# MLA attention: VectorE's work of the maxima in program order, their row on ScalarE's queue, their start one chunk later

## The chip, the cores and the metric

The kernel runs on one core of one Trainium2 chip. The metric is device time in microseconds from launch to end; the program is the same in each run. The profile is one execution of it, recorded on that core; its times count from the start of the span.

## What is computed

The kernel computes two layers over 2048 latent tokens with 256 context tokens ahead of them, width 1024: multi-head latent attention (MLA), then gated linear attention. The change lies in MLA, of which this is the part that matters:

```python
q = (rms_norm(cq, q_norm_g) @ w_uq).reshape(b, n, MLA_HEADS, MLA_NOPE + MLA_ROPE)      # 16 heads, 64 + 32
...
k = jnp.concatenate([k_nope, jnp.broadcast_to(kr, (b, n, MLA_HEADS, MLA_ROPE))], axis=-1)
...
s = jnp.einsum('bqhrd,bkhd->bhrqk', qi, k, preferred_element_type=F32) * scale
p = jax.nn.softmax(s, axis=-1).astype(v.dtype)
return jnp.einsum('bhrqk,bkhe->bqhre', p, v)
...
return (o.reshape(b, n, MLA_WIDTH) * jax.nn.silu(gate)) @ w_out
```

Context queries read the 256 context keys only; latent queries read all 2304 keys.

## The kernel before

**Tiling.** Heads go in 8 pairs, and each pair's queries in 5 chunks: the context (256 columns) and four of 512. `steps` lists the 40 (pair, chunk) in order, and `si` is an index in it. Keys come in tiles of 128, so an *item* (si, kt) is one tile of keys against one chunk of queries for two heads: 2 items for a context chunk, 18 for each other, 74 for a pair, 592 in all.

**The maxima run ahead.** Softmax needs each query's maximum before its scores are exponentiated. `maxima()` is a generator, advanced step by step: one step is four matmuls of 128 queries against up to 512 keys (L491) into two of the three PSUM banks of pool `pmp` (tile `pmx`) and two reductions on VectorE (L493) into the tile `mx`; a chunk of 512 columns takes 20 steps, a context chunk 2. When a chunk is complete, `close()` reduces `mx` to `mc` (L502, VectorE), transposes it on TensorE (L505), writes the negative as `mr` (L509, VectorE) and sends it with two small DMAs (L511) into row 32 of that chunk's query tile `qs`. There it is the 33rd row of the last of five terms of the scores, against a row of ones in the keys.

**Query up-projection (p2q, 535 to 690 us).** Five chunks, each of 8 pairs and 4 rope blocks; a block is nine matmuls into a `pj` bank. `feed()` advances the maxima here until 30 steps (`lead`) are done; its step `due` and the places that call it set where they fall. The function `fetch()` prepares the first query and key tiles between them: a DMA, then two GpSimd instructions that split the tile in a high and a low part (L48, L53).

**Attention (p3, 690 to 2366 us).** One loop over the items. Each item has `scores` (ten matmuls L628 into one of two PSUM tiles `st`, then Exp on ScalarE L630 into one slot of a ring of nine) and mostly one step of the maxima; one item in three prepares a key or query tile of what comes later. Behind each group of up to six items comes a *burst*: `thirds` sums three slots on VectorE in four instructions (L661), `values` multiplies the group's slots with `vt` (L677, 24 matmuls for six items), `finish` ends the chunk that was completed in the burst before (L692 on TensorE over the sums `acc`, Ln and Exp on ScalarE, a product on GpSimd, a DMA), `gated` (L683, VectorE) takes over the output of a chunk whose last group this was, and a chunk whose maxima are complete is closed: mc ahead of the thirds, the transpose and mr behind the values. GpSimd adds slots and sums up in `acc` (L651). In the last pair the loop also prepares the output weights `wo` (cast on ScalarE, low part on VectorE or GpSimd) and the first context output `o0h`, `o0l`.

**What sets the order.** A scheduler orders each engine's program. An instruction that went through `tc.keep_in_program_order` stays behind the one traced just before it on its engine; `pe_op` does this once `pinned` is set, at the start of p3. In p3 the matmuls, the reductions L493 and the thirds L661 are pinned; mc, mr and ob (L683) are not. DMAs wait in the program of the engine that issues them, in its order; those of L511 are issued by SyncE, as are the loads of qf, kf, gt and vt.

Of the kernel before, what the change touches and what calls it, by code (L numbers as in the profile page):

```python
# [10 lines left out]
F32 = mybir.dt.float32  # L11
F32R = mybir.dt.float32r
# [110 lines left out]
def body(ctx, tc, I, out, stop=99, dbg=None):  # L123
# [349 lines left out]
    def maxima():  # L473

        for si, (pr, ci) in enumerate(steps):
# [3 lines left out]
            qs = qss[si]  # L479
            mx = qsp.tile([P, 8, 5], F32, name="mx", bufs=2)  # L480
            kh = kb[pr % 2][0]
# [16 lines left out]
    def close(si, qs, mx, nq, npart):  # L498

        n = nq * P  # L500
        mc = qsp.tile([P, 8], F32, name="mc", bufs=2)
        nc.vector.reduce_max(mc[:, :2 * nq], mx[:, :2 * nq, :npart], axis=AX.X)  # L502
        yield
        pt = pmp.tile([P, 512], F32, name="pmx")
        pe_op(nc.tensor.transpose(pt[:2 * nq, :P], mc[:, :2 * nq], ident))  # L505
        yield
        closed.add(si)
        mr = qsp.tile([8, P], F32R, name="mr", bufs=2)
        nc.vector.tensor_scalar(mr[:2 * nq, :], pt[:2 * nq, :P], -1.0, None, op0=ALU.mult)  # L509
        for j in range(2):  # L510
            nc.sync.dma_start(qs[64 * j + 32:64 * j + 33, 1, 1, :n].bitcast(F32), mr[j * nq:j * nq + nq, :].bitcast(F32))  # L511

# [7 lines left out]
    with pool("p2q", 2) as sp, pool("ps2q", 5, space=PSUM) as psp:  # L520
# [20 lines left out]
        def feed():  # L541
            nonlocal fed, due
            due += 0.82
            while fed < min(due, lead):
                fed += 1
                next(stream, None)
                while closes:
                    for _ in closes.pop():
                        pass

        for ci, (c0, n) in enumerate(CHUNKS):
# [4 lines left out]
            if ci == 3:  # L556
                tasks.append((load_q, (2,)))
            for pr in range(NPAIR):
                if pr == 1 and ci + 1 < len(CHUNKS):
# [9 lines left out]
                store(qn_d[ci][pr], kk[:, :n])  # L569
                if ci >= 3 or (ci == 2 and pr >= 4):  # L570
                    feed()
            tab = sp.tile([P, 2, 512], F32, name="tabq", bufs=1)
            nc.sync.dma_start(tab[:, :, :n], I["tab"][:, :, c0:c0 + n])
            for g in range(2):
# [6 lines left out]
                for r in range(2):  # L581
# [6 lines left out]
                    store(qr_d[ci][4 * g:4 * g + 4, :, 16 * r:16 * r + 16, :].rearrange("q h d t -> (q h) d t"), t1[:, :n])  # L588
                    if ci >= 2:
                        feed()  # L590
                        feed()
# [8 lines left out]
    wo = {}  # L600
    tc.keep_in_program_order(nc.scalar.preload_act_table_set("natural_log_exp_and_others"))
    with pool("p3", 2) as sp, pool("ps3", 2, space=PSUM) as psp:
# [76 lines left out]
        def gated(si):  # L679
            n = CHUNKS[steps[si][1]][1]  # L680
            st_ = live[si]
            st_["ob"] = sp.tile([P, 512], F32, name="ob")
            nc.vector.tensor_tensor(st_["ob"][:, :n], st_["po"][:, :n], st_["gt"][:, :n], op=ALU.mult)  # L683

# [25 lines left out]
        def first_o():  # L710
# [3 lines left out]
            oh, ol = [qsp.tile([P, KT, P], F32R, name=f"o0{s}", tag="qf", bufs=2) for s in "hl"]  # L714
            k.hi("a", oh, of)
            k.lo("v", ol, of, oh)
            return oh, ol
# [24 lines left out]
        def out_weights(b, raw):  # L742
# [3 lines left out]
            for kt in range(4):  # L746
                k.hi("a", w2[0][:, kt, :], raw[kt])
                k.lo("p" if kt == 2 else "v", w2[1][:, kt, :], raw[kt], w2[0][:, kt, :])
                wo[4 * b + kt] = (w2[0][:, kt, :], w2[1][:, kt, :])
# [8 lines left out]

        def burst(i, end=False):

            nonlocal nv, nb, fed
            group = items[nv:i]
            nv = i
            nb += 1
# [25 lines left out]
        for i, (si, kt, nk) in enumerate(items):  # L790
# [19 lines left out]
            if i == len(items) - 30:  # L810
                o0 = first_o()
            if i and (items[i - 1][1] % 6 == 5 or items[i - 1][1] == items[i - 1][2] - 1):
                burst(i)
        burst(len(items))
        out_weights(1, raw)
# [747 lines left out]
```

## Time and profile before

| | us |
|---|---|
| median of 3 runs | 3736.59 |
| lowest, highest | 3736.35, 3737.76 |
| the profiled execution | 3737.41 |
| its span | 3735.6 |
| TensorE busy | 3539.5 |
| VectorE busy | 2283.1 |
| ScalarE busy | 1336.9 |
| GpSimd busy | 1405.8 |

The span is what the profile shows of an execution; 1.8 us of the profiled one lie outside it. In the rows, PE is TensorE's matmul, PEld its weight load, DVE VectorE, ACT ScalarE, POOL GpSimd, SP SyncE; SPq and ACTq are DMAs issued by these. A name as `pmx<-kbs,qs` reads output<-inputs, and L491 is line 491. An idle time in square brackets is that of the engine just before the row, with what released it. A row of windows is a stretch and its length, then busy time (and instructions) of PE, PEld, DVE, ACT and POOL, of PE and PEld alone where a line of TensorE's is picked, and then the granted clock of TensorE as a share of full speed, the busy share of the DMA engines, and GB/s.

### The profile page before, as it was taken

The numbers are of one execution on the slowest core, as the hardware profiler recorded it, in microseconds if no ns is written. First come the engines' busy times: TensorE is split into PE (matmuls) and PEld (weight loads), VectorE is DVE, ScalarE is ACT, GpSimd is POOL, SyncE is SP. The second block draws the span as 40 slices with busy tenths as digits, with TensorE's granted clock in tenths as the row PEclk, the third lists the DMA queues.
The fourth block names the chain that finished last, engine by engine and source line by source line (L and its number), as shares of the span: only waits on it lengthen the run. The fifth ranks groups of instructions, "written<-read, shape, count | busy, mean of one in ns | idle before, by whom it ended". The sixth has DMA issues, their size and how long they took to land.

```text
span 3735.6 us, 59336 instructions
## 1 busy us (share of the span) xinstructions
PE 3539.5 (95%) x24126; PEld 2665.9 (71%) x24126; DVE 2283.1 (61%) x3356; ACT 1336.9 (36%) x1951; POOL 1405.8 (38%) x867
## 2 busy tenths in 40 slices
PE   6999999899999999999989989999999999999799
PEld 5777886556556666566656655677999899999677
DVE  4333324577776777777767766464266787777863
ACT  2232221234333343343334434332234454444431
POOL 3111214366675666667576646655000101000000
PEclk9999999999999999999999989999999999999899
DMA  6121455402111111202110010477675766668432
GB/s 229 67 78 50 159 202 168 124 24 81 45 39 59 49 49 46 68 24 79 43 52 20 22 42 10 141 238 235 242 249 186 243 204 214 230 208 293 144 130 96
DMA packets 280922, 456.02 MB, mean 122 GB/s; under 512 B 23028, under 2 KB 179764, under 8 KB 268680
## 3 DMA queue, kind: packets, MB, share of 16 engines
q1 hardware_dynamic: 216312, 375.21, 30.5%
q10 hardware_dynamic: 64336, 77.02, 6.0%
q8 instruction: 189, 3.10, 0.3%
q14 instruction: 85, 0.70, 0.1%
HBM read 311.27 MB, written 140.71 MB: 121 GB/s over the span
## 4 chain that ended last, share of the span: by engine, by line
PE 71%; DMA 7%; DVE 7%; issue 7%; POOL 5%; ACT 2%; SPq 1%; ACTq 0%; POOLq 0%; DVEq 0%
PE st L628 16%; PE po L677 12%; PE pmx L491 7%; PE pj L60 4%; PE pj L61 4%; PE pj L62 4%; PE pp L981 3%; PE pp L983 3%; PE pp L982 3%; POOL acc L651 2%; DVE part L661 1%; PE pg L1219 1%; PE py L981 1%; PE py L983 1%; PE py L982 1%
## 5 line engine op out<-in xcount | busy, mean ns | idle before, releaser
L493 DVE TENSOR_REDUCE mx<-pmx 128x1 f32<-128x512 f32 (+1 forms) x1312 | 767.1, 627 | 338.0 <-PE pmx L491 328.5
L651 POOL TENSOR_TENSOR acc<-acc,pe 128x1024 f32<-128x1024 f32 x288 | 688.7, 2391 | 526.6 <-DVE acc L661 318.6
L630 ACT ACTIVATE pe<-st 128x1024 f32<-128x1024 f32 (+1 forms) x592 | 600.3, 1014 | 754.5 <-PE st L628 697.6
L628 PE MATMUL st<-qs,kbs 64*128 64x512 f32 (+3 forms) x5920 | 811.2, 393 | 24.7 <-DMA qs<-mr 15.3
L628 PEld LDWEIGHTS st<-qs,kbs 64*128 64x128 f32 (+1 forms) x5920 | 590.4, 187 | 131.5 <-DMA qs<-mr 16.2
L677 PE MATMUL po<-pe,vt 128*64 128x512 f32 (+1 forms) x2368 | 527.2, 594 | 5.9 <-DMA vt<-v_d 5.9
L491 PE MATMUL pmx<-kbs,qs 64*128 64x512 f32 (+1 forms) x2624 | 448.1, 385 | 49.9 <-DVE mx L493 40.8
L491 PEld LDWEIGHTS pmx<-kbs,qs 64*128 64x128 f32 x2624 | 275.0, 189 | 175.4 <-DVE mx L493 64.1
L677 PEld LDWEIGHTS po<-pe,vt 128*64 128x64 f32 x2368 | 161.6, 137 | 317.4 <-issue 305.1
L981 PE MATMUL pp<-w,ht 128*128 128x256 f32 x1088 | 317.7, 292 | 0.0
L982 PE MATMUL pp<-w,ht 128*128 128x256 f32 x1088 | 305.9, 281 | 0.0
L983 PE MATMUL pp<-w,ht 128*128 128x256 f32 x1088 | 304.9, 280 | 0.0
L1330 POOL TENSOR_TENSOR orr<-oss,mhalf 128x4 f32<-128x4 f32 x16 | 17.1, 1067 | 655.1 <-DVE oss L1329 655.1
L661 DVE TENSOR_REDUCE part<-pe 128x256 f32<-128x768 f32 x256 | 249.4, 1028 | 22.7 <-ACT pe L630 22.6
L981 PEld LDWEIGHTS pp<-w,ht 128*128 128x128 f32 x1088 | 205.5, 189 | 3.5
L982 PEld LDWEIGHTS pp<-w,ht 128*128 128x128 f32 x1088 | 205.7, 189 | 1.1
L983 PEld LDWEIGHTS pp<-w,ht 128*128 128x128 f32 x1088 | 205.4, 189 | 0.1
L981 PE MATMUL pp<-ht,w 128*128 128x256 f32 (+1 forms) x616 | 183.1, 298 | 10.2 <-ACT vge L1046 7.9
L982 PE MATMUL pp<-ht,w 128*128 128x256 f32 (+1 forms) x616 | 175.1, 284 | 0.0
L983 PE MATMUL pp<-ht,w 128*128 128x256 f32 (+1 forms) x616 | 174.6, 283 | 0.1
L119 POOL TENSOR_TENSOR rs_r<-rs_v,mhalf 128x1 f32<-128x1 f32 x52 | 29.2, 562 | 382.1 <-DVE rs_v L117 382.1
L1205 ACT ACTIVATE ex<-df 128x512 f32<-128x512 f32 x192 | 114.2, 632 | 145.5 <-DVE df L1202 126.7
(370 smaller groups left out, 6299.0 us busy)
## 6 DMA issues: line engine op xcount, KB each, us to landing
ht<-hh_d SPq DMA_DIRECT2D x44, 1024.0 KB
ht<-hl_d SPq DMA_DIRECT2D x44, 1024.0 KB
xt<-in_x SPq DMA_DIRECT2D x32, 512.0 KB
mod_w<-in_ada_w SPq DMA_DIRECT2D x16, 1024.0 KB
v<-gv_d SPq DMA_DIRECT2D x32, 512.0 KB
wsg<-in_gla_w_in SPq DMA_DIRECT2D x66, 192.0 KB
v_d<-vs ACTq DMA_DIRECT2D x18, 512.0 KB
vt<-v_d SPq DMA_DIRECT2D x8, 1152.0 KB
```

What stands on the lines that cost most here:

```text
L60: nc.tensor.matmul(ps, ah, bh, start=(i == 0), stop=False)
L61: nc.tensor.matmul(ps, ah, bl, start=False, stop=False)
L491: pe_op(nc.tensor.matmul(ps[j][:, :w], qs[js, 0, i, t * P:t * P + P], kk[js, bs], start=(i == 0), stop=(i == 1)))
L493: pe_op(nc.vector.reduce_max(mx[:, j * nq + t, b:b + 1], ps[j][:, :w], axis=AX.X))
L628: pe_op(nc.tensor.matmul(st[:, j, :n], a[js, ks], qs[js, s, r, :n], start=(i == 0), stop=(i == len(terms) - 1)))
L630: nc.scalar.activation(pe[:, :, :n], st[:, :, :n], AF.Exp, scale=SCALE)
L651: nc.gpsimd.tensor_tensor(acc, acc, part, op=ALU.add)
L661: pe_op(nc.vector.tensor_reduce(part[:, j, c:c + 256], src, axis=AX.X, op=ALU.add))
L677: pe_op(nc.tensor.matmul(po[64 * j:64 * j + 64, :n], vt[:, kt, 64 * j:64 * j + 64], pe[:, j, :n], start=(kt == 0), stop=(kt == nk - 1)))
L981: nc.tensor.matmul(ps, ah, bh, start=(i == 0), stop=False)
L982: nc.tensor.matmul(ps, ah, bl, start=False, stop=False)
L983: nc.tensor.matmul(ps, al, bh, start=False, stop=(i == n - 1))
```

## The change

Six things are altered. (1) mc, mr and ob are pinned in p3, with four tiles `mx` for two and three `mc` and `mr` for two. (2) In p3 the two DMAs of mr are issued by ScalarE. (3) The maxima are fed from the fourth chunk of p2q on (ci 3), not from the second half of the third; `due` grows by 0.96 a call, not 0.82, and 30 steps are done as before. (4) The table for Exp is loaded at the start of p2q's last chunk and not behind p2q. (5) The bursts have a table of their own: the group of a context chunk (2 items) has its burst three items later, and with it the finish of the chunk before. (6) In the last pair the casts and low parts of o0 and wo are pinned, and all low parts of wo are GpSimd's.

```diff
-            mx = qsp.tile([P, 8, 5], F32, name="mx", bufs=2)
+            mx = qsp.tile([P, 8, 5], F32, name="mx", bufs=4)
...
-        mc = qsp.tile([P, 8], F32, name="mc", bufs=2)
-        nc.vector.reduce_max(mc[:, :2 * nq], mx[:, :2 * nq, :npart], axis=AX.X)
+        mc = qsp.tile([P, 8], F32, name="mc", bufs=3)
+        pe_op(nc.vector.reduce_max(mc[:, :2 * nq], mx[:, :2 * nq, :npart], axis=AX.X))
...
-        mr = qsp.tile([8, P], F32R, name="mr", bufs=2)
-        nc.vector.tensor_scalar(mr[:2 * nq, :], pt[:2 * nq, :P], -1.0, None, op0=ALU.mult)
+        mr = qsp.tile([8, P], F32R, name="mr", bufs=3)
+        pe_op(nc.vector.tensor_scalar(mr[:2 * nq, :], pt[:2 * nq, :P], -1.0, None, op0=ALU.mult))
         for j in range(2):
-            nc.sync.dma_start(qs[64 * j + 32:64 * j + 33, 1, 1, :n].bitcast(F32), mr[j * nq:j * nq + nq, :].bitcast(F32))
+            (nc.scalar if pinned else nc.sync).dma_start(qs[64 * j + 32:64 * j + 33, 1, 1, :n].bitcast(F32), mr[j * nq:j * nq + nq, :].bitcast(F32))
...
-            due += 0.82
+            due += 0.96
...
+            if ci == 4:
+                tc.keep_in_program_order(nc.scalar.preload_act_table_set("natural_log_exp_and_others"))
...
-                if ci >= 3 or (ci == 2 and pr >= 4):
+                if ci >= 3:
                     feed()
...
-                    if ci >= 2:
+                    if ci >= 3:
                         feed()
                         feed()
...
-    tc.keep_in_program_order(nc.scalar.preload_act_table_set("natural_log_exp_and_others"))
...
-            nc.vector.tensor_tensor(st_["ob"][:, :n], st_["po"][:, :n], st_["gt"][:, :n], op=ALU.mult)
+            pe_op(nc.vector.tensor_tensor(st_["ob"][:, :n], st_["po"][:, :n], st_["gt"][:, :n], op=ALU.mult))
...
-            k.hi("a", oh, of)
-            k.lo("v", ol, of, oh)
+            tc.keep_in_program_order(k.hi("a", oh, of))
+            tc.keep_in_program_order(k.lo("v", ol, of, oh))
...
-                k.hi("a", w2[0][:, kt, :], raw[kt])
-                k.lo("p" if kt == 2 else "v", w2[1][:, kt, :], raw[kt], w2[0][:, kt, :])
+                tc.keep_in_program_order(k.hi("a", w2[0][:, kt, :], raw[kt]))
+                tc.keep_in_program_order(k.lo("p", w2[1][:, kt, :], raw[kt], w2[0][:, kt, :]))
...
+        bursts = {i + (4 if nk == 2 else 1): i + 1 for i, (si, kt, nk) in enumerate(items) if kt % 6 == 5 or kt == nk - 1}
+
-            group = items[nv:i]
-            nv = i
+            group = items[nv:bursts[i]]
+            nv = bursts[i]
...
-            if i and (items[i - 1][1] % 6 == 5 or items[i - 1][1] == items[i - 1][2] - 1):
+            if i in bursts:
                 burst(i)
```

Three places show what moves. The first is VectorE's row at the first closing of the attention loop, that of the maxima of pair 0's second chunk of 512. Here `mx<-pmx` is the reduction of a maxima matmul's bank, `acc` and `part` are thirds. Before:

```order
L493 TENSOR_REDUCE mx<-pmx 128x1 x12
L661 TENSOR_REDUCE acc<-pe 128x256 x4
L493 TENSOR_REDUCE mx<-pmx 128x1 x6
L502 TENSOR_REDUCE mc<-mx 128x8
L661 TENSOR_REDUCE part<-pe 128x256 x3
L493 TENSOR_REDUCE mx<-pmx 128x1 x2
L661 TENSOR_REDUCE part<-pe 128x256
L493 TENSOR_REDUCE mx<-pmx 128x1 x6
L509 TENSOR_SCALAR mr<-pmx 8x128
```

After:

```order
L493 TENSOR_REDUCE mx<-pmx 128x1 x6
L662 TENSOR_REDUCE acc<-pe 128x256 x4
L493 TENSOR_REDUCE mx<-pmx 128x1 x14
L502 TENSOR_REDUCE mc<-mx 128x8
L662 TENSOR_REDUCE part<-pe 128x256 x4
L509 TENSOR_SCALAR mr<-pmx 8x128
L493 TENSOR_REDUCE mx<-pmx 128x1 x14
```

Before, mc and three of four instructions of a third stand amid the reductions of maxima, and mr behind six more of them. After, mc stands behind all that were traced ahead of it, the four of the third are together, and mr is next.

The second is TensorE's row at the start of a pair (pair 4): `st` of 256 columns are the scores of the context chunk, `po` the values, and L692 (L693 after) is the finish, 512 columns wide for the last chunk of the pair before. Before:

```order
L677 MATMUL po<-pe,vt 64x512 x12
L491 MATMUL pmx<-kbs_3831,qs 128x512 x4
L628 MATMUL st<-qs,kbs_3831 128x256 x10
L491 MATMUL pmx<-kbs_3831,qs 128x256 x4
L628 MATMUL st<-qs,kbs_3831 128x512 x10
L677 MATMUL po<-pe,vt 64x256 x4
L692 MATMUL pmx<-acc,ones 64x512 x2
L491 MATMUL pmx<-kbs_3831,qs 128x512 x4
L628 MATMUL st<-qs,kbs_3831 128x512 x10
L491 MATMUL pmx<-kbs_3831,qs 128x512 x4
```

After:

```order
L629 MATMUL st<-qs,kbs_3831 128x256 x10
L491 MATMUL pmx<-kbs_3831,qs 128x256 x4
L629 MATMUL st<-qs,kbs_3831 128x512 x10
L491 MATMUL pmx<-kbs_3831,qs 128x512 x4
L629 MATMUL st<-qs,kbs_3831 128x512 x10
L491 MATMUL pmx<-kbs_3831,qs 128x512 x4
L629 MATMUL st<-qs,kbs_3831 128x512 x10
L491 MATMUL pmx<-kbs_3831,qs 128x512 x4
L629 MATMUL st<-qs,kbs_3831 128x512 x10
L491 MATMUL pmx<-kbs_3831,qs 128x512 x4
L678 MATMUL po<-pe,vt 64x256 x4
L693 MATMUL pmx<-acc,ones 64x512 x2
```

The values of the context chunk and the finish behind them stood one item of scores behind the context's own scores of the second tile; now they stand four items behind, three more than before.

The third is the row of maxima at the start of pair 6. SyncE's queue before:

```order
L435 DMA kf<-k_d 128x512
L449 DMA qf<-qn_d 128x512
L452 DMA qf<-qr_d 32x512 x4
L435 DMA kf<-k_d 128x512
L449 DMA qf<-qn_d 128x256
L452 DMA qf<-qr_d 32x256 x4
L606 DMA vt<-v_d 128x18x128
L511 DMA qs<-mr 1x4x128 x2
L620 DMA gt<-gate_d 128x512
```

ScalarE's row after, at the same place (`pe<-st` is the Exp; of the size 128x2x256 are those of the context chunk):

```order
L695 ACTIVATE rs<-pmx 128x512
L696 ACTIVATE rs<-rs 128x512
L631 ACTIVATE pe<-st 128x1024 x11
L631 ACTIVATE pe<-st 128x2x256
L511 DMA qs<-mr 1x4x128 x2
L631 ACTIVATE pe<-st 128x2x256
L631 ACTIVATE pe<-st 128x1024 x4
L695 ACTIVATE rs<-pmx 128x512
```

Before, the row of maxima stood behind loads of qf, kf and vt. After, it stands on ScalarE between the two Exp of the context chunk, and nothing of L511 is left on SyncE in p3.

## Rows read from the trace of the kernel before

**Rows 1.** The page: busy time of TensorE, and the chain that ended last.

```profile
PE 3539.5 (95%) x24126; PEld 2665.9 (71%) x24126; DVE 2283.1 (61%) x3356; ACT 1336.9 (36%) x1951; POOL 1405.8 (38%) x867
...
PE 71%; DMA 7%; DVE 7%; issue 7%; POOL 5%; ACT 2%; SPq 1%; ACTq 0%; POOLq 0%; DVEq 0%
```

**Rows 2.** Windows, four chunks of the query projection; then line 491 (maxima) alone.

```profile
549.00:573.50 24.50, 24.50 (x110) 20.19 (x109) 7.79 (x16) 4.70 (x8) 7.53 (x11) 1.00 0.67 207
573.50:618.10 44.60, 36.66 (x145) 26.01 (x143) 19.09 (x32) 4.59 (x8) 23.68 (x22) 0.85 0.53 171
618.10:656.90 38.80, 38.80 (x162) 24.82 (x161) 22.56 (x38) 4.69 (x8) 16.19 (x16) 1.00 0.43 131
656.90:689.60 32.70, 32.70 (x144) 22.64 (x143) 16.35 (x29) 4.69 (x8) 10.49 (x8) 1.00 0.42 132
...
573.50:618.10 44.60, 7.99 (x34) 4.60 (x34) 0.85 0.53 171
618.10:656.90 38.80, 11.94 (x53) 5.47 (x52) 1.00 0.43 131
```

**Rows 3.** Timeline at two of TensorE's waits, and a window around the first.

```profile
596.11 1.22 PE L491 MATMUL pmx<-kbs,qs 64*128 64x256 f32 x6 [7.94 <-POOL qs L48]
...
703.82 1.98 PE L677 MATMUL po<-pe,vt 128*64 128x256 f32 x8 [5.90 <-DMA vt<-v_d]
...
590.00:600.00 10.00, 3.89 (x12) 2.70 (x13) 1.67 (x5) 1.17 (x2) 3.09 (x4) 0.52 0.70 244
```

**Rows 4.** Waits of TensorE in attention: us in total, times, longest.

```profile
PE pmx L491 <- DVE mx L493: 40.8, 34, 2.2
PE pmx L692 <- POOL acc L651: 16.1, 6, 4.8
PE st L628 <- DMA qs<-mr: 15.3, 2, 8.8
PE st L628 <- ACT pe L630: 9.3, 2, 7.6
```

**Rows 5.** Timeline at a closing of maxima; windows from burst to burst.

```profile
929.13 0.60 PE L692 MATMUL pmx<-acc,ones 128*64 128x256 f32 x4
...
934.27 0.20 DVE L502 TENSOR_REDUCE mc<-mx 128x8 f32<-128x40 f32 x1
934.38 2.93 DVE L661 TENSOR_REDUCE part<-pe 128x256 f32<-128x768 f32 x3
...
937.96 0.72 PE L491 MATMUL pmx<-kbs,qs 64*128 64x512 f32 x3 [1.51 <-DVE mx L493]
...
923.93:941.91 17.98, 16.21 (x115) 10.10 (x113) 16.03 (x23) 6.66 (x8) 12.46 (x6) 1.00 0.03 9
941.91:957.40 15.49, 15.49 (x116) 9.84 (x115) 7.50 (x14) 6.21 (x7) 8.60 (x5) 1.00 0.01 2
```

**Rows 6.** Timeline at the start of a pair.

```profile
912.72 1.08 PE L692 MATMUL pmx<-acc,ones 128*64 128x512 f32 x4 [2.30 <-POOL acc L651]
```

**Rows 7.** Timeline at the row of maxima, pair 6; SyncE's row of pair 7.

```profile
1945.53 0.27 DVE L509 TENSOR_SCALAR mr<-pmx 8x128 fp32r<-8x128 f32 x1
...
1951.25 2.57 SPq L511 DMA_DIRECT2D qs<-mr  x2
...
1956.95 0.99 PE L628 MATMUL st<-qs,kbs 33*128 33x512 f32 x2 [8.79 <-DMA qs<-mr]
...
2161.78 1.24 SPq L511 DMA_DIRECT2D qs<-mr  x2
```

**Rows 8.** Timeline at the cast of o0 on ScalarE.

```profile
2199.30 1.04 ACT L46 CAST o0h<-of 128x1024 fp32r<-128x1024 f32 x1 [8.21 <-DMA of<-o_d]
...
2201.32 2.50 PE L628 MATMUL st<-qs,kbs 64*128 64x512 f32 x10 [7.58 <-ACT pe L630]
```

**Rows 9.** VectorE's waits for the transpose, in attention; an Exp in the timeline.

```profile
DVE mr L509 <- PE pmx L505: 82.1, 29, 5.6
...
936.25 1.02 ACT L630 ACTIVATE pe<-st 128x1024 f32<-128x1024 f32 x1 [0.59 <-PE st L628]
```

More of the change, by code (lines that the diff above doesn't have):

```diff
@@ L757, in body, with burst @@
         done, extra, nv, nb = [], mods(), 0, 0
-        def burst(i, end=False):
+        bursts = {i + (4 if nk == 2 else 1): i + 1 for i, (si, kt, nk) in enumerate(items) if kt % 6 == 5 or kt == nk - 1}
+        def burst(i):
             nonlocal nv, nb, fed
-            group = items[nv:i]
-            nv = i
+            group = items[nv:bursts[i]]
+            nv = bursts[i]
             nb += 1
@@ L811, in body @@
                 o0 = first_o()
-            if i and (items[i - 1][1] % 6 == 5 or items[i - 1][1] == items[i - 1][2] - 1):
+            if i in bursts:
                 burst(i)
+        assert nv == len(items) - 6 and max(bursts) == len(items)
         burst(len(items))
```

## The prediction, made before the changed kernel ran

> **What bounds the kernel now.** I read the page first. TensorE is busy for 3539.5 of 3735.6 us and holds 71% of the chain that ended last [rows 1], so an edit on another engine pays only where TensorE stands, and the sum below is a list of TensorE's stands. Nothing that TensorE computes is removed: its instructions are the same in number. Then I read the stage of the diff: four stretches of the query up-projection, one chunk of queries each [rows 2], the stands in and just behind it [rows 3], TensorE's waits in attention, 687 to 2420 us [rows 4], and around each kind of wait the timeline [rows 5 to 9]. In attention VectorE is the releaser of most: 40.8 us in 34 waits of a maxima matmul for a reduction that frees its PSUM bank. Then come 16.1 us for GpSimd's accumulation, 15.3 us in two waits for the row of maxima, and 9.3 us for ScalarE [rows 4].
>
> **A, maxima begin later.** The first of the four stretches has no maxima and lasts 24.50 us; the third has 53 maxima matmuls and lasts 38.80, so a matmul of maxima costs (38.80 - 24.50) / 53 = 0.27 us. By that price the second, with 34, should last 33.7 and lasted 44.60: 10.9 us too many [rows 2]. They are one stand of 7.94 us for the query tile that GpSimd prepares, and the ten microseconds around it had a granted clock of 0.52 [rows 3]. After the change this stretch has no maxima. The 30 steps of four matmuls fall into the next two: 15 in the third, 11 in the fourth, 4 behind the last projection instead of 1. Sum: 24.5 + (24.5 + 60 x 0.27) + (24.5 + 44 x 0.27) = 101.6, and 3 steps more behind it 3.2, so 104.8 against 44.60 + 38.80 + 32.70 = 116.1: -11.3. The table for Exp moves one chunk forward; of the two waits of scores for ScalarE in [rows 4] one is the cast of E (7.6); the other, 9.3 - 7.6 = 1.7 us, stood while that table was loaded and the first exponentials ran, so -1.7. I take **-13**. Bounds: the 5.90 us stand for the values' tile vt [rows 3] stays, and may swallow the 3.2 us (-16), or the rope that ends the stage comes some 2.5 us later by its place behind the maxima and moves it (-10); two more if the clock or the table turn out otherwise: -6 to -17. The query tile was there at 596.1 and the third stretch, which would begin at 573.5 + 24.5 = 598.0, asks for it some steps later, so the stand doesn't move there.
>
> **B, mc held in place.** When a chunk's maxima are complete, the small reduction mc is traced at the burst of values. It was free to move, and the scheduler put it ahead of reductions of maxima that TensorE waits for; the sums of three ring slots (part), which are pinned to what is traced ahead of them, came along. In the timeline mc and three parts take 934.27 to 937.31, and the maxima matmul stands 1.51 us [rows 5]. Of the waits over 0.3 us in attention 17 have such a row ahead of them, 6 have the modulation's copy mod_s, which stays, one the low part of o0. Price of one: the stretch between two bursts lasts 17.98 against 15.49 us; 0.60 of the difference is a finish (L692): 2.49 - 0.60 = 1.9; TensorE's own idle time is 17.98 - 16.21 = 1.77 [rows 5]. The 17 stretches against their unstalled neighbours, summed, give 43 us, 2.5 each, since some hold two such waits. I take 2.2, between: 17 x 2.2 = **-37**, from 17 x 1.77 = -30 to -43. Now mc and the parts stand behind all reductions traced earlier. What is late next is the parts, by a reduction or two of 0.65 us; they free ring slots, of which there are nine.
>
> **C, the context's values four items later.** At each start of a pair the previous pair's last sums were wanted while GpSimd was still adding: the wait of 2.30 us at 912.72 [rows 6]. The line has 16.1 us in six waits; without the last, 4.8, which is at the end, 11.3 in five [rows 4]. Three items of scores now lie between; an item with its maxima is some 1.6 us, so 4.8 us of cover over 2.3. With the slower matmuls behind: **-12** (-9 to -13).
>
> **D, the row of maxima on ScalarE's queue.** In pair 6 mr was ready at 1945.80, and the row was issued only at 1951.25, since SyncE's queue stood behind the loads of a query tile and of vt; the scores stood 8.79 us for it [rows 7]. The other wait is 15.3 - 8.79 = 6.5 us [rows 4, 7]. From ScalarE's queue it goes out when mr is done. TensorE went on 5.7 us after the first issue (1956.95 - 1951.25); with the two issues in 1.24 us, as in pair 7, and not 2.57, that is 4.4 [rows 7]. So it would have gone on at 1950.2, 2.0 us after its stand began (1956.95 - 8.79 = 1948.16): (8.8 - 2.0) + (6.5 - 2.0) = 11.3, **-11** (-6 to -13). What is queued behind these issues is the next Exp.
> A rule of the Trainium skill speaks against this edit: "DMA: Bandwidth & Descriptors", section "Issuing engines are not separate DMA queues", says that another issuing engine saves no more than the sequencer's time to initiate a transfer, usually small beside the transfer. By that rule the gain would be the issue alone, 1.24 us at each stand, and D would be -2.5. The trace disagrees for this case, since 5.45 us of the 8.79 were the row standing in SyncE's program behind other issues, not the transfer.
>
> **E, pinned casts of o0.** ScalarE's cast stood 8.21 us for its load, with Exp behind it, and scores stood 7.58 and then ran 2.50 instead of 1.33 us [rows 8]. The cast now stands 34 items later, long after the load: -9. o0's low part, moved likewise, held up maxima by up to 2.2 us [rows 4]: together **-11** (-8 to -12).
>
> **F, the end.** The low parts of the output weights leave VectorE, whose additions beside GpSimd's made the last accumulation late; of the 4.8 us at the end [rows 4] I take **-1.6**. GpSimd now does four low parts there, ahead of its share of the output projection: +4 at most, so -2 to +4.
>
> **G, what is added.** 38 closings issue two small DMAs each on ScalarE: 1.24 us a pair by the row of pair 7, 2.57 with the time between them by that of pair 6 [rows 7]. Exp takes 1.02 us and ScalarE idles 0.59 before the next [rows 9]; scores are double-buffered; at a closing the row goes out while TensorE computes the first scores behind the burst. So a single closing costs nothing and five double ones about 0.7 each: **+4**. Lower bound 0; with no cover 38 x 1.24 = +47.
> mr is now pinned too. VectorE waited for the transpose 29 times, 82.1 us [rows 9], so mr is not late by itself; queued behind it are only reductions whose matmuls stand behind that transpose.
>
> **Sum.** -13 - 37 - 12 - 11 - 11 - 1.6 + 4 = -81.6. The profiled execution took 3737.41, 3735.6 of it span; 3737.4 - 81.6 = 3655.8, and since the median is 3736.59, 0.8 lower: **3655 us**.
>
> **Rivals.**
> 1. The queue of ScalarE takes back half. If the row's issues are not covered, G is +47 and not +4: 3655 + 43 = 3698. For it: the idle 0.59 us of a step is less than 1.24. Against: two score tiles in PSUM. Much the same would come of B's wait moving on and not going, 3655 + 37 = 3692. I give it 0.25, spread over 3670 to 3710.
> 2. Slower: ScalarE, in order, stands for mr at each closing. If VectorE arrives at mr late, its four sums (2.93 / 3 x 4 = 3.9 us, [rows 5]) and the issues (1.24) lie ahead of Exp; with 1.6 us of cover by the second score tile that is 3.9 + 1.24 - 1.6 = 3.5 us, 38 x 3.5 = 133, and 3655 + 133 = 3788. It decides from (81.6 / 38) = 2.15 us a closing. For it: an engine on the path now waits for another, 38 times. Against: VectorE waited 82.1 / 29 = 2.8 us for the transpose; it would have to be some 5 us later than now. 0.08.
> 3. The closings aren't the cause, and the stands appear elsewhere, since VectorE does the same work in the same stretches: within 7.5 us of before, 3737. Against: the stretch without a closing in [rows 5] has TensorE busy for all of its 15.49 us. 0.05.
>
> **How the numbers follow.** About 0.2%, 7.5 us, is what a measurement of this kernel can tell from no change. The forecast, 3640 to 3670, has 0.60, with 0.02 for a still larger gain (the clock dips behind removed stands). Faster is the forecast, that larger gain and rival 1: 0.87; same 0.05; slower 0.08. The bounds of the terms, taken together at their good ends, are -17 - 43 - 13 - 13 - 12 - 2 = -100, so 3636; low is 3632. To hold 8 in 10 the range must reach over most of rival 1: high 3698.
>
> **What would show it.** In the changed kernel: the second stretch of the projection as short as the first, at clock 1.00 (A); the line of maxima matmuls for VectorE down from 40.8 to some 12, what mod_s leaves (B); the line for GpSimd's accumulation under 5 (C); that for the row near 5 in two waits (D); ScalarE's line near 0 (E). Wrong it is if scores wait for ScalarE's Exp at closings (rivals 1 and 2), or if the maxima still wait behind parts.

## The result, and the profile of the changed kernel

The changed kernel takes 3641.89 us (median of 4, 3639.85 to 3651.36), the kernel before 3736.47: a ratio of 0.9747, interval 0.9729 to 0.9764, or 95 us less. The profiled execution took 3641.14, its span is 3639.3. 3655 was forecast.

The page, busy time and the chain that ended last, beside [rows 1]:

```profile
PE 3512.7 (97%) x24126; PEld 2657.4 (73%) x24126; DVE 2266.6 (62%) x3350; ACT 1337.6 (37%) x1951; POOL 1418.4 (39%) x873
...
PE 78%; DMA 6%; issue 6%; DVE 5%; POOL 3%; ACT 2%; SPq 1%; ACTq 0%; POOLq 0%; DVEq 0%
```

TensorE is busy for 26.8 us less with the same instructions, and its share of the chain rose from 71% to 78%. So the span lost two things: 69.5 us in which TensorE stood, and 26.8 in which it did the same work more slowly. The waits of TensorE in attention (us in total, times, longest), beside [rows 4]:

```profile
PE pmx L491 <- DVE mx L493: 10.0, 10, 1.7
PE pmx L693 <- POOL acc L652: 3.1, 1, 3.1
PE py L62 <- POOL ol L53: 1.7, 1, 1.7
PE st L629 <- DMA qs<-mr: 1.2, 1, 1.2
PE py L60 <- POOL oh L48: 1.2, 1, 1.2
PE st L629 <- ACT pe L631: 0.2, 1, 0.2
```

The maxima wait 10.0 us and not 40.8, the sums 3.1 and not 16.1, the row 1.2 and not 15.3, scores for Exp 0.2 and not 9.3. What is new stands in the rows of `py`, the output projection.

Where the 96.3 us of span went, by stretches that hold the same work of TensorE in both kernels (us). Here p3 is from the first scores to the first product of the output projection, and it is divided at the start of the ninth item's scores: by then 156 matmuls of maxima and the values of the context chunk are done in both. The first values would not do as a border, since after the change three more items of scores stand ahead of them.

| stretch | before | after | difference |
|---|---|---|---|
| start to query projection | 535.2 | 534.0 | -1.2 |
| query projection | 155.1 | 154.6 | -0.4 |
| p3, first scores to the ninth item | 25.8 | 14.9 | -10.9 |
| p3, the rest | 1651.7 | 1556.4 | -95.3 |
| output projection of MLA | 224.9 | 230.2 | +5.4 |
| the second layer | 1143.0 | 1149.2 | +6.2 |

The second layer is the same code in all kernels here, and takes 1142 to 1158 us in their profiles, without order; its 6.2 us are no part of the change. TensorE in the rest of p3, before and after (length, busy time, granted clock):

```profile
716.03:2367.73 1651.70, 1571.91 (x11041) 0.98 0.14 43
703.48:2259.87 1556.39, 1542.79 (x11040) 1.00 0.15 47
```

Its idle time falls from 79.8 to 13.6 us, by 66, and its busy time by 29 for the same matmuls. Before, the granted clock was at half in 57 us of this stretch, after in 7.

I then took each of the 103 stretches from burst to burst with its excess over the pace of undisturbed ones (0.116 us a matmul of scores or maxima, 0.22 of values): 104.5 us in all before, 9.1 after. By what TensorE waited for in them: VectorE's reductions 55 before and 13 after, the row of maxima 20.5 and 1.3, o0 13.2 and 0, the pair starts 12.5 and 0. The rest of the difference, 8.5 us, is spread.

A closing in the timeline of the changed kernel, the one that answers to [rows 5]:

```profile
916.32 1.29 DVE L493 TENSOR_REDUCE mx<-pmx 128x1 f32<-128x512 f32 x2 [0.34 <-PE pmx L491]
...
917.53 0.18 DVE L502 TENSOR_REDUCE mc<-mx 128x8 f32<-128x40 f32 x1
917.63 3.85 DVE L662 TENSOR_REDUCE part<-pe 128x256 f32<-128x768 f32 x4
...
922.69 0.27 PE L505 MATMUL pmx<-ident,mc 128*8 128x128 f32 x1
...
923.00 0.28 DVE L509 TENSOR_SCALAR mr<-pmx 8x128 fp32r<-8x128 f32 x1 [1.52 <-PE pmx L505]
923.31 1.22 ACTq L511 DMA_DIRECT2D qs<-mr  x2
...
924.89 1.03 ACT L631 ACTIVATE pe<-st 128x1024 f32<-128x1024 f32 x1 [6.31 <-DMA qs<-mr]
```

mc stands behind the reductions, the four thirds behind mc beside the values, and mr behind the transpose; no maxima matmul stands. The row goes out at once, and the next Exp begins 0.4 us behind the issues. VectorE, done with the four sums, waits 1.52 us for the transpose; in all of attention (beside [rows 9]):

```profile
DVE mr L509 <- PE pmx L505: 26.2, 29, 2.1
```

As often as before, but 26.2 us and not 82.1: VectorE now comes to mr later, and still not last.

### The profile page after: what moved, and what is told of

Same layout as the page of the kernel before. It is cut to its first block, busy times and chain, and to the rows that moved or that the text cites. A ratio compares the mean times of both kernels' runs of the same rounds, so it can differ in the third digit from the quotient of the medians.

```text
span 3639.3 us, 59322 instructions
## 1 busy us (share of the span) xinstructions
PE 3512.7 (97%) x24126; PEld 2657.4 (73%) x24126; DVE 2266.6 (62%) x3350; ACT 1337.6 (37%) x1951; POOL 1418.4 (39%) x873
## 4 chain that ended last, share of the span: by engine, by line
PE 78%; DMA 6%; issue 6%; DVE 5%; POOL 3%; ACT 2%; SPq 1%; ACTq 0%; POOLq 0%; DVEq 0%
PE st L629 18%; PE po L678 14%; PE pmx L491 8%; PE pj L60 5%; PE pj L62 4%; PE pj L61 4%; PE pp L985 3%; PE pp L986 3%; PE pp L987 3%; DMA wsg<-in_gla_w_in 2%; PE py L62 2%; PE py L61 2%; PE py L60 2%; PE pk L1152 1%; PE py L985 1%
## 5 line engine op out<-in xcount | busy, mean ns | idle before, releaser
L629 PE MATMUL st<-qs,kbs 64*128 64x512 f32 (+3 forms) x5920 | 801.9, 390 | 1.5 <-DMA qs<-mr 1.2
L491 PE MATMUL pmx<-kbs,qs 64*128 64x512 f32 (+1 forms) x2624 | 435.4, 380 | 14.2 <-DVE mx L493 13.9
L985 PE MATMUL pp<-ht,w 128*128 128x256 f32 (+1 forms) x616 | 182.9, 297 | 10.8 <-ACT vge L1050 9.1
```

The lines of the kernel that those rows point to most:

```text
L491: pe_op(nc.tensor.matmul(ps[j][:, :w], qs[js, 0, i, t * P:t * P + P], kk[js, bs], start=(i == 0), stop=(i == 1)))
L629: pe_op(nc.tensor.matmul(st[:, j, :n], a[js, ks], qs[js, s, r, :n], start=(i == 0), stop=(i == len(terms) - 1)))
L985: nc.tensor.matmul(ps, ah, bh, start=(i == 0), stop=False)
```

## Experiments

Five kernels are the kernel before with one part of the change alone, and e6_tiles has only the tiles of the first part; the others alter the changed kernel, b3_all in two things and b4_all in three. "p3" is the time from the first scores to the first product of the output projection in the kernel's trace: 1677.5 us before, 1571.3 after. It comes from one execution of each; how much it varies between executions was not measured. The kernel before took from 3731 to 3754 us in its runs, so a few us in p3 are weak evidence by themselves.

| kernel | median, us | ratio to before, interval | p3 |
|---|---|---|---|
| e1_pins | 3697.47 | 0.9888, 0.9864 to 0.9912 | 1632.5 |
| e2_row_act | 3724.33 | 0.9959, 0.9947 to 0.9971 | 1659.9 |
| e3_bursts | 3723.98 | 0.9952, 0.9935 to 0.9970 | 1656.4 |
| e4_p2q | 3731.64 | 0.9975, 0.9958 to 0.9991 | 1665.7 |
| e5_casts | 3723.30 | 0.9954, 0.9936 to 0.9972 | 1648.3 |
| e6_tiles | 3738.54 | 0.9990, 0.9980 to 0.9999 | 1673.6 |
| u1_row_sp | 3647.92 | 0.9752, 0.9738 to 0.9767 | 1579.9 |
| c1_row_x2 | 3676.03 | 0.9827, 0.9809 to 0.9845 | 1607.7 |
| c2_row_x1 | 3634.27 | 0.9701, 0.9686 to 0.9715 | 1563.5 |
| b1_feed | 3639.13 | 0.9730, 0.9715 to 0.9745 | 1570.7 |
| b3_all | 3626.58 | 0.9684, 0.9670 to 0.9698 | 1557.4 |
| b4_all | 3620.19 | 0.9668, 0.9643 to 0.9693 | 1556.5 |

Three theories stood against each other. Theory 1: the slower matmuls behind a stand belong to it and go with it. Theory 2: the prices of the forecast. Theory 3: the slower matmuls come back only when all stands are gone.

### The pins alone, and the tiles alone

e1_pins:

```diff
-        nc.vector.reduce_max(mc[:, :2 * nq], mx[:, :2 * nq, :npart], axis=AX.X)
+        pe_op(nc.vector.reduce_max(mc[:, :2 * nq], mx[:, :2 * nq, :npart], axis=AX.X))
...
-        nc.vector.tensor_scalar(mr[:2 * nq, :], pt[:2 * nq, :P], -1.0, None, op0=ALU.mult)
+        pe_op(nc.vector.tensor_scalar(mr[:2 * nq, :], pt[:2 * nq, :P], -1.0, None, op0=ALU.mult))
```

with ob pinned likewise and the numbers of tiles of the change. Expected:

> The kernel before with mc, mr and ob pinned and the additional tiles for mx, mc and mr, and nothing else; the row of maxima stays on SyncE's queue. Theory 1 (what the stretches of the traces say: the stand and the slower matmuls behind it belong to one place and go with it): the stretches between bursts with a wait of maxima for VectorE exceeded their pace by 61 us before and 13 after, so -48, about 3688. Theory 2 (the forecast's price, 2.2 us for each of 17): -37, about 3699. Theory 3 (the slower matmuls only come back when all stands are gone together): idle time alone, 17 x 1.77 = -30, about 3706. TensorE's waits for maxima fall from 40.8 to 10 to 12 us in all three.

e6_tiles:

```diff
-            mx = qsp.tile([P, 8, 5], F32, name="mx", bufs=2)
+            mx = qsp.tile([P, 8, 5], F32, name="mx", bufs=4)
...
-        mc = qsp.tile([P, 8], F32, name="mc", bufs=2)
+        mc = qsp.tile([P, 8], F32, name="mc", bufs=3)
...
-        mr = qsp.tile([8, P], F32R, name="mr", bufs=2)
+        mr = qsp.tile([8, P], F32R, name="mr", bufs=3)
```

Expected:

> The kernel before with the additional tiles alone (mx 4, mc and mr 3) and nothing pinned. If the pins did the work of the first experiment (theory 1): 0, about 3740, with TensorE's waits for the maxima still near 40 us. If the tiles did it (reductions run ahead because their target is free): -45, about 3697.

The pins took 45 us off p3, the tiles 4. TensorE's waits from the projection to the output projection with the pins:

```profile
PE pmx L692 <- POOL acc L651: 15.3, 6, 4.8
PE pmx L491 <- DVE mx L493: 11.5, 9, 2.2
PE st L628 <- DMA qs<-mr: 9.8, 1, 9.8
...
PE pmx L491 <- DVE mr L509: 7.2, 1, 7.2
```

With the tiles alone:

```profile
PE pmx L491 <- DVE mx L493: 41.2, 33, 2.2
```

So the pins remove the stands behind mc. That the pin of mc does it is argued from the rows; mc, mr and ob were not pinned one by one. Of the 45 us, TensorE's idle time is 29 (from 79.8 to 50.3 from the first values on), which theory 3 had for the whole; the other 15 were slower matmuls, which came back though the stands of the other parts were still there. By time, 0.9888 is -42, with an interval of -33 to -51. Theory 3 (30) falls. The interval holds theory 1 (48 as expected, 42 by the count above) and the forecast (37), and doesn't decide between them. The clock is a small part of it: from the first values on the time lost to a granted clock under 1.00 is 31.5 us before and 28.0 with the pins. The larger part is at full clock; two groups of ten scores in the kernel before, ahead of the stand at 937.96 and behind it:

```profile
931.85 1.35 PE L628 MATMUL st<-qs,kbs 64*128 64x512 f32 x10
...
938.29 1.55 PE L628 MATMUL st<-qs,kbs 64*128 64x512 f32 x10
```

In a stretch at clock 1.00 [rows 5] the second takes 0.2 us more. The pins alone also show what the forecast did not have: a maxima matmul waits 7.2 us for mr. The timeline there, in pair 7:

```profile
2107.32 3.86 DVE L661 TENSOR_REDUCE part<-pe 128x256 f32<-128x768 f32 x4
...
2111.10 5.57 DVE L53 TENSOR_TENSOR wo<-wso,wo 128x1024 fp32r<-128x1024 f32 x2
...
2117.19 0.27 DVE L509 TENSOR_SCALAR mr<-pmx 8x128 fp32r<-8x128 f32 x1
...
2117.52 1.81 PE L491 MATMUL pmx<-kbs,qs 64*128 64x512 f32 x4 [7.22 <-DVE mr L509]
```

mr, pinned behind the four sums, stands on VectorE also behind two low parts of the output weights, 5.57 us, and the transpose holds one of the three banks until then. In the changed kernel, where another part of the change gives these low parts to GpSimd, mr begins at most 0.45 us behind its transpose at each of the 38 closings.

### The row's queue: alone, taken back, doubled and halved

e2_row_act, the kernel before with

```diff
-            nc.sync.dma_start(qs[64 * j + 32:64 * j + 33, 1, 1, :n].bitcast(F32), mr[j * nq:j * nq + nq, :].bitcast(F32))
+            (nc.scalar if pinned else nc.sync).dma_start(qs[64 * j + 32:64 * j + 33, 1, 1, :n].bitcast(F32), mr[j * nq:j * nq + nq, :].bitcast(F32))
```

> The kernel before with the row of maxima on ScalarE's queue in attention and nothing else; mr is not pinned. Theory 1: the two stretches with the wait for the row exceeded their pace by 9.7 + 9.5 us, and the one behind the first by 1.4, and this falls to 1.3: -19, about 3717. Theory 2: -11 for the stands and +4 for 76 issues: about 3729. If ScalarE's issues are not covered, +47 less 11 to 19: about 3765.

u1_row_sp is the changed kernel with that line as before:

> The changed kernel with the row of maxima back on SyncE's queue. Theory 1: +19 us (the two waits and the slow stretches return), about 3661. Theory 2: +11 - 4 = +7, about 3649. Rival: pinned mr alone had removed the waits, since SyncE's queue is ready sooner: 0.

Alone the edit takes 17.6 us off p3 and 15 off the time (0.9959); taken back from the changed kernel it costs 8.6 us in p3, and in time no difference is clear (0.9752 against 0.9747, with overlapping intervals). The timeline of u1_row_sp at the start of pair 6:

```profile
1877.80 0.27 DVE L509 TENSOR_SCALAR mr<-pmx 8x128 fp32r<-8x128 f32 x1
...
1884.37 0.38 SPq L607 DMA_DIRECT2D vt<-v_d  x1
1884.85 2.51 SPq L511 DMA_DIRECT2D qs<-mr  x2
...
1890.43 1.00 PE L629 MATMUL st<-qs,kbs 33*128 33x512 f32 x2 [9.98 <-DMA qs<-mr]
```

mr is ready at 1878.07, the loads of qf and vt stand ahead of the row until 1884.85, and the scores stand 9.98 us, just as in [rows 7]. The second wait, in pair 7, is not there: it came of the loads of the output weights, which in the kernel before held SyncE from 2153.47 to 2161.68 us, and the pinned casts move these away (in e5_casts the row is issued 0.3 us behind mr). So the two waits had two causes: the pinned casts also remove the second, and only the first needs this edit. In the changed kernel the same place:

```profile
1880.68 0.27 DVE L509 TENSOR_SCALAR mr<-pmx 8x128 fp32r<-8x128 f32 x1
1880.98 2.43 ACTq L511 DMA_DIRECT2D qs<-mr  x2
...
1884.49 0.50 PE L629 MATMUL st<-qs,kbs 33*128 33x512 f32 x1 [1.17 <-DMA qs<-mr]
```

mr is ready at 1880.95, issued at 1880.98, and the scores stand 1.17 us and not 8.79. This bears on the rule of the Trainium skill ("DMA: Bandwidth & Descriptors", section "Issuing engines are not separate DMA queues"), by which only the time of the issue would be saved. The traces disagree with it here. The time from the first issue to TensorE's next matmul is 3.5 us on ScalarE's queue and 5.6 on SyncE's; 6.8 us more were the row standing in SyncE's program.

c1_row_x2, the changed kernel with four issues a closing, and c2_row_x1 with one:

```diff
+            for h in range(2):
+                hq = nq // 2
+                (nc.scalar if pinned else nc.sync).dma_start(qs[64 * j + 32:64 * j + 33, 1, 1, h * hq * P:(h + 1) * hq * P].bitcast(F32), mr[j * nq + h * hq:j * nq + (h + 1) * hq, :].bitcast(F32))
```

```diff
-        for j in range(2):
-            (nc.scalar if pinned else nc.sync).dma_start(qs[64 * j + 32:64 * j + 33, 1, 1, :n].bitcast(F32), mr[j * nq:j * nq + nq, :].bitcast(F32))
+        (nc.scalar if pinned else nc.sync).dma_start(qs[32:97:64, 1, 1, :n].bitcast(F32), mr[:2 * nq, :].bitcast(F32))
```

> The changed kernel with each small DMA of the row of maxima cut in two: four issues and not two at each closing, 76 more on ScalarE's queue in attention. If the issues are covered (theory 1: no stretch of the changed kernel shows a wait for Exp): 0 to +4. If issues cost what the forecast put for double closings, 0.7 for each of a few: +4. If they are not covered: 38 x 1.24 = +47.

> The changed kernel with the row of maxima sent by one DMA for both heads and not by two: one issue of 0.6 us on ScalarE at each closing. If two issues are covered in the changed kernel (theory 1): 0, within 4 us. If they already cost half of what two further ones cost in c1_row_x2 (+36 us for 76): -18 and more.

Two issues more cost 36 us in p3, and some 30 by time (0.9827 against 0.9747), most of the 47 of the forecast's first rival; theory 1 had said 0 to 4 and was wrong. Waits of TensorE, and the timeline of c1_row_x2 at a place where two chunks close together:

```profile
PE st L631 <- ACT pe L633: 13.1, 20, 2.4
...
PE st L631 <- DMA qs<-mr: 7.5, 4, 6.0
```

```profile
1636.79 4.95 ACTq L513 DMA_DIRECT2D qs<-mr  x8
...
1642.14 1.94 ACT L633 ACTIVATE pe<-st 128x1024 f32<-128x1024 f32 x2 [10.32 <-DMA qs<-mr]
...
1643.22 1.43 PE L631 MATMUL st<-qs,kbs 64*128 64x512 f32 x10 [2.43 <-ACT pe L633]
```

There the eight issues hold ScalarE for 4.95 us, two Exp come late, and scores stand 2.43. Of the 36 us, 22 are idle time of TensorE. One issue less gains 7.8 us in p3 (1571.3 to 1563.5): 1.7 ahead of the first values, and of the other 6.0 only 2.2 are idle time, half of it the rest of the row's stand. By time it gains 8 us by the medians and 17 by the ratios (0.9701 against 0.9747, with intervals that don't overlap). So the "0, within 4 us" of theory 1 is wrong here too, and by the ratios the "-18 and more" of the other expectation is nearly reached. With the other repairs below in, it gains 0.8 in p3, and in time no difference is clear (b4_all against b3_all). So four issues a closing are not covered, and two are not quite; how much the second costs, between almost nothing and 17 us, stays open.

### The bursts alone

```diff
-            if i and (items[i - 1][1] % 6 == 5 or items[i - 1][1] == items[i - 1][2] - 1):
+            if i in bursts:
```

with the table `bursts` of the change.

> The kernel before with the table of bursts alone (values of the context chunk, and the finish before them, three items later). Theory 1 and 2: -12, about 3724; theory 3: the idle time of the five waits, -11. The line of L692 for GpSimd's accumulation falls from 16.1 us to the 4.8 at the end. If three items later collide with the closing that stands there: less than -5.

0.9952 is -18 us, 21 in p3. The line of the pair starts is gone:

```profile
PE pmx L692 <- POOL acc L651: 4.8, 1, 4.8
```

What is left is the end. Of the 9 us above the forecast, 5.9 are the wait for vt at the first burst of all [rows 3], which is later here and doesn't wait: the forecast had taken that stand as staying.

### The projection alone, and its start moved

e4_p2q has the later feed and the earlier table load alone:

> The kernel before with the later feed of the maxima and the earlier table load alone. Theory 1 (from the trace after: the stand in the projection moved to the next chunk and shrank from 7.9 to 3.9 + 1.2 us, the stretch up to the first scores is as long as before, the first values come 3 us sooner): -4, about 3732. The forecast: -13, about 3723.

0.9975 is -9 us, between the two. In its trace the projection takes 155.1 us, as before, the stretch from the first scores to the first values 5.4 and not 13.6. What changed there is the load of vt. SyncE before, and then in the changed kernel:

```profile
673.23 22.84 SPq L452 DMA_DIRECT2D qf<-qr_d  x8
696.17 0.39 SPq L606 DMA_DIRECT2D vt<-v_d  x1
...
685.73 0.39 SPq L607 DMA_DIRECT2D vt<-v_d  x1
```

vt stands behind loads of qf, which wait for the ropes of the projection. With the later feed alone it is issued at 688.31 and not at 696.17, and the first values wait 1.65 us for it and not 5.90; in the changed kernel they don't wait. Why the loads of qf go out sooner was not tested. In the changed kernel the chunks of the projection, beside [rows 2]:

```profile
571.73:596.41 24.68, 24.68 (x109) 20.19 (x108) 10.43 (x14) 4.60 (x8) 16.49 (x16) 1.00 0.82 261
596.41:642.96 46.55, 41.39 (x164) 26.53 (x162) 23.27 (x39) 4.70 (x8) 23.95 (x22) 0.89 0.44 136
642.96:684.60 41.64, 41.14 (x170) 25.53 (x169) 23.56 (x42) 5.98 (x9) 10.99 (x9) 1.00 0.38 114
```

The first of these is as short as forecast (24.68), the next 46.55 where 40.7 was forecast, at a clock of 0.89, and the last 41.64 where 36.4 was, since it holds more of the maxima. The stand in the second of them:

```profile
602.26 0.69 DVE L587 TENSOR_TENSOR t<-pj,tabq 128x512 f32<-128x512 f32 x1 [7.01 <-POOL t L588]
...
605.08 0.74 DVE L493 TENSOR_REDUCE mx<-pmx 128x1 f32<-128x256 f32 x2
605.55 0.79 PE L491 MATMUL pmx<-kbs,qs 64*128 64x256 f32 x3 [3.91 <-DVE mx L493]
```

VectorE's rope product waits 7.01 us for GpSimd's part of the rope, which stood behind the preparation of the query tile; the reduction of the maxima stands behind it on VectorE, and TensorE waits 3.91. So the stand of 7.94 us became 3.91 and moved on: by these rows it is GpSimd's backlog, not only the query tile's arrival. b1_feed begins two projections later:

```diff
-            due += 0.96
+            due += 1.0
...
-                if ci >= 3:
+                if ci >= 4 or (ci == 3 and pr >= 2):
                     feed()
```

> The changed kernel with the maxima fed from the third pair of the fourth chunk on (two projections later), 30 steps done as before. Theory 1 (the stand of 3.9 us is a reduction that waits behind rope, whose GpSimd part waits behind the preparation of the query tile): the first maxima come after that, the stands of 3.9 and 1.2 us and the clock of 0.72 to 0.77 behind them go: -8, about 3634. If the stand moves again with the first maxima: 0.

The stand moved again:

```profile
609.20 1.74 DVE L53 TENSOR_TENSOR cl<-cq,ch 128x512 fp32r<-128x512 f32 x1 [0.51 <-POOL ch L48]
...
611.33 0.49 PE L491 MATMUL pmx<-kbs,qs 64*128 64x256 f32 x3 [3.26 <-DVE mx L493]
```

The projection takes 155.1 us, and the ratio of 0.9730 can't be told from the changed kernel's. VectorE is busy here with splits that wait for GpSimd, wherever the maxima begin. A kernel without GpSimd's backlog at this place wasn't tried, so that it is the cause of the whole stand is argued from the rows and not shown.

### The casts and low parts alone

```diff
-            k.hi("a", oh, of)
-            k.lo("v", ol, of, oh)
+            tc.keep_in_program_order(k.hi("a", oh, of))
+            tc.keep_in_program_order(k.lo("v", ol, of, oh))
...
-                k.lo("p" if kt == 2 else "v", w2[1][:, kt, :], raw[kt], w2[0][:, kt, :])
+                tc.keep_in_program_order(k.lo("p", w2[1][:, kt, :], raw[kt], w2[0][:, kt, :]))
```

> The kernel before with the casts and low parts of o0 and of the output weights pinned, all low parts of the weights on GpSimd, and nothing else. Theory 1: the two stretches with o0's waits exceeded their pace by 9.0 + 4.2 us: -13, and -2 at the last finish; the output projection starts later behind GpSimd's low parts, two waits of 1.2 and 1.7 us with a slower clock: +5. Net -10, about 3726. Forecast: -11 - 1.6, about 3724.

0.9954 is -17 us, 29 in p3, and the output projection is slower (228.6 us against 224.9). The waits:

```profile
PE st L628 <- DMA qs<-mr: 9.0, 1, 9.0
...
PE st L628 <- ACT pe L630: 1.7, 1, 1.7
```

Scores wait for the cast no more, and one of the two waits for the row is gone too, the one of pair 7: 9.5 us of the 29 that e2_row_act also has. The five parts alone take 125 us off p3 and together 106. Those 9.5 are half of this overlap. Another 5.5 lie at the wait for vt, which e3_bursts and e4_p2q both shorten: from the start of the query projection to the ninth item e3_bursts is 6.0 us shorter than the kernel before, e4_p2q 10.8, and the changed kernel 11.3.

### What the rows pointed to

In the changed kernel's timeline at the end:

```profile
2258.77 9.40 POOL L53 TENSOR_TENSOR wo<-wso,wo 128x1024 fp32r<-128x1024 f32 x4
2258.86 1.08 PE L693 MATMUL pmx<-acc,ones 128*64 128x512 f32 x4 [3.12 <-POOL acc L652]
...
2274.01 0.51 PE L60 MATMUL py<-wo,oh 128*128 128x512 f32 x1 [1.15 <-POOL oh L48]
...
2276.45 0.50 PE L62 MATMUL py<-wo,ol 128*128 128x512 f32 x1 [1.70 <-POOL ol L53]
```

GpSimd's four low parts take 9.40 us, its cast of the next output comes late, and the output projection waits 1.15 and 1.70 us. b3_all gives two of them to VectorE, and moves the bias addition of the modulation from VectorE, where it waits for ScalarE ahead of the maxima, to GpSimd:

```diff
-                tc.keep_in_program_order(k.lo("p", w2[1][:, kt, :], raw[kt], w2[0][:, kt, :]))
+                tc.keep_in_program_order(k.lo("p" if b == 0 or kt > 1 else "v", w2[1][:, kt, :], raw[kt], w2[0][:, kt, :]))
...
-    nc.vector.tensor_tensor(m[0:2, :], m[0:2, :], bias, op=ALU.add)
+    (nc.gpsimd if callable(pt) else nc.vector).tensor_tensor(m[0:2, :], m[0:2, :], bias, op=ALU.add)
```

> The changed kernel with two of the last four low parts of the output weights on VectorE again, and the addition of the bias to mod_s (L79) on GpSimd in attention. The first aims at the start of the output projection, where two waits of 1.2 and 1.7 us for GpSimd and slow matmuls behind cost 4.5 us: -4. The second at the six or so waits of the maxima behind mod_s, 13 us above their pace in the changed kernel: -10 if VectorE's wait for ScalarE's copy is the cause, 0 if it is the PSUM bank that the modulation holds. Together about 3628 or 3638.

```profile
PE pmx L491 <- DVE mx L493: 5.8, 5, 4.0
```

The maxima wait 5.8 us, nearly all in the projection; p3 from the first values on is 1547.1 and not 1561.0 us, and the output projection 224.4 and not 230.2: -13.9 and -5.8. That speaks for VectorE's place in the row as the cause of the wait behind mod_s, and against the PSUM bank, for which 0 was expected. The two edits were made in one kernel, so they are told apart by stretch alone. b4_all adds the single DMA of c2_row_x1:

> b3_all with the row of maxima in one DMA as in c2_row_x1. If the second issue on ScalarE costs by itself (attention 1561 to 1555 us in c2_row_x1): attention falls from 1547 to about 1541 us, the time to some 3620. If that gain came from the same stretches as that of b3_all: attention stays at 1547. A ratio to the kernel before of about 0.967.

From the first values on p3 stays at 1546.0 us, so the gain of the single DMA came from stretches that b3_all has repaired. At 0.9668 b4_all is ahead of both kernels; from b3_all (0.9684) it can't be told.

## Why the prediction was right, step by step

The way and the range were right; the size was 82 us where 95 came. Term by term, from the traces:

- **A**, -13 forecast, -11.3 measured from the start of the query projection to the ninth item (-0.4 and -10.9 in the table). The size is near by luck. Up to the first scores 11.3 us were to go, and 0.4 went. The step that failed is "so the stand doesn't move there": the query tile was there in time, but the rope behind its preparation on GpSimd was late, VectorE with it, and the reduction behind that. The stand came back with half its length, and the chunks that took over the maxima grew. What was gained instead is the wait of 5.90 us for vt, of which the forecast says "stays": vt was issued 10.4 us sooner. With it went the 1.7 us for Exp, as forecast, a wait of 1.3 us for VectorE, and the slow matmuls behind.
- **B**, -37 forecast, -42 by stretches and -45 in p3 with the pins alone. The cause and the number of places were right. The price was low by the matmuls behind a stand, which run slower; the forecast had taken 2.2 us, below the 2.5 that the 17 stretches gave.
- **C**, -12 forecast, -12.5 by stretches. Alone it gave more, since the wait for vt went with it; in the changed kernel that wait is in A's stretch.
- **D**, -11 forecast, -19 by stretches, -17.6 alone. Mis-sized twice: 2.0 us were to remain of each stand, and 1.17 and 0 remained; and the stretches behind them, with the clock down, were not counted. The cause was right for one of the two waits: the other goes with E's edit as well.
- **E**, -11 forecast, -13.2 by stretches.
- **F**, -1.6 forecast with +4 as its bad end. The last wait fell from 4.8 to 3.1 us, and the output projection grew by 5.4: +3.7, the bad end, by the mechanism named there.
- **G**, +4 forecast. The trace shows no wait for Exp over 0.2 us. The second of the two issues costs between almost nothing and 17 us by the single DMA, so the term is neither shown nor refuted.

The rivals: the first did not come, but it was near. Twice the issues cost 36 us, most of its price, so the argument against it (a second score tile) holds in the main for two issues a closing and not for four. The second did not come: VectorE waits for the transpose at 29 closings as before, and at the other nine mr begins within 0.45 us of it. That a late mr costs is shown, though not on the way by ScalarE: at the one closing of e1_pins where VectorE was late at mr, behind two low parts, TensorE stood 7.2 us for the bank of the transpose. The third fell with e1_pins: held in place, the same work of VectorE leaves 11.5 us of waits for maxima and not 40.8.

In the stages that the change touches the gain was 101 us (-0.4, -106.2 and +5.4), 20 more than the forecast; the 6.2 us of the second layer hid a part of that. Most of the 20 is one thing in several terms: I priced a stand by TensorE's idle time and added little for what follows. From the ninth item on TensorE's idle time fell by 66 us, and the time by 95. Of the 29 between, some 19 are the granted clock, an estimate that counts TensorE's busy time at half clock (45.6 us before, 6.8 after) as twice what it takes at full. The single parts differ in this: from the ninth item on the pins alone took 15 us off the busy time, about 5 of them the clock's, and the pinned casts alone 10, all of them the clock's. So here the short stands behind mc cost matmuls at full clock, for a reason that stays open, and the long stand behind o0's cast cost clock. Each is read from one trace.

## What to carry to other kernels

Where an engine executes in order, one free instruction that drags pinned ones ahead of it can stop another engine time and again; look for what stands just ahead of the late instruction, not at its own length. Price a stand by the stretch around it against an undisturbed one: here the stretches lost 1.4 times the idle time. Compare stretches that hold the same work, not those between instructions of the same name, when the change moves one of these. A DMA moved to a compute engine's queue has a price by its issues: four a closing cost some 30 us more than two here.

## What was not expected of the hardware

Four small DMAs on ScalarE instead of two at each of 38 closings cost 36 us of p3, 0.48 for each further issue, where an issue takes some 0.6: most of it is on the path. And at the place shown a group of ten scores behind a stand took 1.55 us at full granted clock, where its neighbours took 1.35.
